# Values two steps behind their scores in the sliding attention, two taps a turn, sums of the last experts deferred, and three or four column tiles begun on half of the tokens

## The chip, the cores and the metric

The kernel runs on one core of a Trainium2 chip. Its engines are TensorE (PE in the profile, with PEld for its weight loads), VectorE (DVE), ScalarE (ACT), GpSimd (POOL) and SyncE (SP, which issues the DMAs). The metric is device time in microseconds of one execution of the whole program; the number to be compared is the median of the runs.

## The reference

Two transformer layers over 512 tokens of width 1024 run one after the other, all in float32. Cut to what the change touches:

```python
def first_block(x, ...):
    xn = rms_norm(h, g_mix); proj = xn @ w_in          # columns: conv 2*512, q 512, k 128, v 128, two gates of 1024
    conv_o = silu(layer_norm(depthwise_conv(a * sigmoid(gate), 31 taps))) @ w_conv_out
    attn_o = sliding_window_attention(q, k, v, sinks) @ w_attn_out   # 8 heads, 2 kv heads, window 128, blocks of 128
    h = h + (sigmoid(gate_conv) * conv_o + sigmoid(gate_attn) * attn_o) @ w_out
    h = h + hierarchical_moe(rms_norm(h, g_ffn), ...)  # 32 experts of 512, 2 per token
    return rms_norm(h, g_final)                        # and then the second layer:
def hybrid_layer(x, ...):
    h1 = rms_norm(x, mix_norm_gain); proj = h1 @ w_in_2              # gated delta rule and sparse attention
    ...
    x = x + merged @ w_out_2
    gate, up = split(rms_norm(x, ffn_norm_gain) @ w_gate_up_2)       # 2 x 2816 columns
    return x + (silu(gate) * up) @ w_down_2
```

In the sliding attention a block of 128 queries sees its own block of keys and the one before; scores get a bias by distance and a sink, then softmax, then the product with the values. In the experts' layer every token's output is the weighted sum of its two experts.

## The kernel before

The 512 tokens are four tiles of 128. A projection makes one column tile of 128 columns at a time for all 512 tokens: `mm3` (lines 327 to 329) writes every float32 product as three, high by high, high by low, low by high, over eight depth steps, 24 matmuls in all. A weight tile is therefore split ahead of use: ScalarE copies the high part (line 196), VectorE or GpSimd subtracts it from the raw weights (line 214). `plan` lists the column tiles in order; `fill_w` splits as many ahead as `look` says, and `next_w` takes one. Raw weights, splits, activations and experts' weights all live in a pool of 20 slots called `ck`; whoever asks for a slot waits until one is released, and DMAs on SP's queue wait in order. PSUM has eight banks, taken one at a time by `ps`. The program is written in one order; a planner with a cost model then orders each engine's instructions, except where `pe` or `keep_in_program_order` fix it or `issue_after` puts an instruction behind another on its engine.

Sliding attention (`swa`, lines 671 to 740): eight steps, one for each block of queries and half of the heads. `scores` does the products (line 692), bias (694), maximum (696), exponentials with sums (700) and scaling (706); `values` transposes the probabilities (717), copies them (719) and multiplies with the values (722). `values` of a step is issued after the scores of the next. `weave` (line 1368) calls the attention one turn at a time, and after every turn issues `pump` waiting convolution taps (line 572, VectorE, 31 per 128 channels) and one piece of `fill`, 12 matmuls of a projection tile. The fill's gates end in a tanh on ScalarE (line 664). After the attention come eight products with the attention's output weights (`branch`, line 621), each with four more taps if any wait, and then the convolution's norm, which needs the sum over all taps.

Experts (`moe`, lines 983 to 1018): 16 pairs of experts. For pair i the gate and up products run, then the down product of pair i-1 (`down`, which writes its output as high and low parts into the one tile `self.y`), and `combine` adds the output of pair i-2 to the tokens: for each of the four token tiles and two halves of the width two matmuls into a bank, and an addition into `h` on VectorE (line 1225). The weights stream in by DMA, 11 chunks of 1 MB ahead.

Start of the second layer (`block2`, lines 1278 to 1345): the sum of pair 15 runs tile by tile; after tiles 0 and 1 come squares (ScalarE, line 1287), the gain (line 1291), squares again, and `pair(0)`, which makes the product of two root-mean-square factors and multiplies (line 1307); the tiles are then transposed (`turn`, line 374). Tiles 2 and 3 follow; their gain runs on GpSimd. While `pair(1)` is made, `begin(2)` computes the first two column tiles for tokens 0 to 255 only, and `finish` does the other half after tiles 2 and 3 are turned.

Feed-forward start (`ffn_x`, `ffn_t`, `ffn_plan`, lines 1995 to 2032): the same pattern, one token tile at a time behind the output projection: norm (line 2007), turn, and before the last turn `begin(2)`. The raw weights of the first gate and up pair lie in `ck`, those of the later ones in a small pool `wf` of the last stage.

Of the kernel before, what the change touches and what calls it, by code (L numbers as in the profile page):

```python
# [8 lines left out]
F32R = mybir.dt.float32r  # L9
# [6 lines left out]
P = 128  # L16
# [136 lines left out]

AHEAD = 11


class Net:
# [336 lines left out]
    def phase_a(self):  # L494
# [120 lines left out]
        ath, atl = (self.ck([P, 4, 512], F32R) for _ in range(2))  # L615
        self.weave([self.swa(q, kv, ath, atl)], fill, pump=4)

# [53 lines left out]
    def swa(self, q, kv, ath, atl):  # L671
# [9 lines left out]
        def scores(qb, r2):  # L681
            nk = 128 if qb == 0 else 256
            k0 = max(qb - 1, 0) * P
            s = self.small([P, 4, 256], "sc", bufs=2)
            mx, nmx, sm, es = (self.small([P, 4], n) for n in ("mx", "nmx", "sm", "es"))
# [41 lines left out]

        steps = [(qb, r2) for qb in range(NT) for r2 in range(2)]
        prev = None
        for st in steps:  # L730
            s = scores(*st)
            yield
            if prev is not None:
                values(*prev)
                yield
            else:
                for _ in range(3):
                    yield
            prev = st + (s,)
        values(*prev)  # L740

# [241 lines left out]
    def moe(self):  # L983
# [5 lines left out]
        for i in range(16):  # L989
            q = quad[i // 2]  # L990
            back = self.combine(quad[i // 2 - 1], i % 2, ys.pop(i - 2)) if i > 1 else iter(())
            if i % 2 == 0:
# [18 lines left out]
            if i:  # L1011
                ys[i - 1] = self.down(i - 1, hT, quad[(i - 1) // 2])
        hT = self.turned(hms.pop(15))
        for _ in self.combine(quad[7], 0, ys.pop(14)):
            pass
        y = self.down(15, hT, quad[7])
        self.start_b()
        self.block2(quad.pop(7), y)

# [173 lines left out]

    def down(self, i, hT, q):

# [3 lines left out]
        for jj in range(2):  # L1199
# [7 lines left out]
            self.prefetch(self.used + AHEAD)  # L1207
        y = self.y
        for half in range(2):
# [3 lines left out]

    def combine(self, q, j, y, done=None):

        nc = self.nc
        mm = nc.tensor.matmul
        for t in range(NT):
            for half in range(2):
                fs = slice(half * 512, half * 512 + 512)  # L1220
                pc = self.ps()
                l = q["ohT"][:, j, t * P:(t + 1) * P]
                self.pe(mm, pc, l, y[:, 0, fs], start=True, stop=False)
                self.pe(mm, pc, l, y[:, 1, fs], start=False, stop=True)
                nc.vector.tensor_tensor(out=self.h[:, t, fs], in0=self.h[:, t, fs], in1=pc, op=ALU.add)  # L1225
                if half == 0:
                    yield
            if done:
                done(t)
            yield  # L1230
# [46 lines left out]

    def block2(self, q, y):

# [9 lines left out]
        def gained(t):  # L1289
            e = nc.gpsimd if t > 1 else nc.vector  # L1290
            e.tensor_tensor(out=self.h[:, t], in0=self.h[:, t], in1=self.rows[:, 0], op=ALU.mult)

        def pair(t2):

            s, v_, r_ = ss[t2], v[t2], r[t2]
            iv = self.small([P, 2], "iv")
            ts_(out=v_[:, 0], in0=s[:, 0], scalar1=1.0 / D, scalar2=EPS, op0=ALU.mult, op1=ALU.add)
            nc.vector.reciprocal(out=iv, in_=v_[:, 0])
            ts_(out=v_[:, 1], in0=s[:, 1], scalar1=1.0 / D, scalar2=None, op0=ALU.mult)
            nc.vector.tensor_tensor(out=v_[:, 1], in0=v_[:, 1], in1=iv, op=ALU.mult)  # L1300
            ts_(out=v_[:, 1], in0=v_[:, 1], scalar1=EPS, scalar2=None, op0=ALU.add)
            self.rsqrt(v_, r_)
            r12 = self.small([P, 2], "r12")
            nc.vector.tensor_tensor(out=r12, in0=r_[:, 0], in1=r_[:, 1], op=ALU.mult)
            for u in range(2):
                x, t = xs[t2][:, u], 2 * t2 + u
                last = nc.vector.scalar_tensor_tensor(out=x, in0=self.h[:, t], scalar=r12[:, u:u + 1], in1=self.rows[:, 1],
                                                      op0=ALU.mult, op1=ALU.mult)
            return self.root, last
# [3 lines left out]
        def done(t):  # L1313
            if t > 1:
                with self.tc.issue_after(first[0].ins):
                    squares(t, 0)
                gained(t)
                return
# [5 lines left out]

        for _ in self.combine(q, 1, y, done=done):
            pass
        self.fill_w()
        for t in (0, 1):
            last = self.turn(xs[0][:, t], t)
        with self.tc.issue_after(last[0].ins):  # L1330
            for t in (2, 3):
                squares(t, 1)
        with self.tc.issue_after(last[1].ins):
            pair(1)
        finish = self.begin(2)
        for t in (2, 3):
# [673 lines left out]
    def ffn_t(self, t):  # L2010
        if t == 1:
            self.look = 1
            self.fill_w()
            self.look = 0
        finish = self.begin(2) if t == NT - 1 else None
        self.turn(self.xs_of[t], t)
# [4 lines left out]
    def ffn_plan(self):  # L2021
# [3 lines left out]
        def wtile(f, a, box={}):  # L2025
            if a == 0:
                box["w"] = w = self.small([P, 2, KD, P], "wf") if f else self.ck([P, 2, KD, P])
                for b in range(2):
# [154 lines left out]
```

## Time and profile before

| what | value |
| --- | --- |
| median of 3 runs | 1784.6 us (1783.42 to 1784.62) |
| profiled execution, its own time | 1785.45 us |
| its span, first to last instruction | 1783.7 us |
| TensorE busy | 1716.4 us, 96% |
| VectorE, ScalarE, GpSimd busy | 827.6, 561.3, 332.4 us |
| mean granted TensorE clock | 0.985 of full speed |

The profile is of one execution. A row of idle time names the engine and line that released the waiting instruction. The granted clock is a share of 2.4 GHz; 0.50 is the lower level of 1.2 GHz, and a window with a value between the two holds both. Matmuls overlap at their ends, so the busy time of a stretch divided by its matmuls, and not the duration of one, is the pitch.

### The profile page before, as it was taken

Reading aid. Unit: us, or ns where it says so; the run is one execution under the profiler, and the core shown is the slowest. Engines: PE = TensorE matmul, PEld = TensorE weight load, DVE = VectorE, ACT = ScalarE, POOL = GpSimd, SP = SyncE. Lnnn points to the kernel's source line nnn. Section 1 sums busy time; section 2 is a strip of 40 time slices with the busy share of each in tenths; the row PEclk is TensorE's granted clock in tenths of the full one; section 3 lists DMA queues with packets and bytes.
Section 4 is the critical chain, followed back from the end, with each engine's and each line's share of the span. In section 5 each row is a group of like instructions: output and inputs, shape, how many; then the busy total and the mean of one; then the engine's idle time right before and its main releaser. Section 6 shows DMA issues by size and latency. Waiting matters only on the chain.

```text
span 1783.7 us, 21733 instructions
## 1 busy us (share of the span) xinstructions
PE 1716.4 (96%) x8672; PEld 1224.0 (69%) x8672; DVE 827.6 (46%) x1516; ACT 561.3 (31%) x1052; POOL 332.4 (19%) x208
## 2 busy tenths in 40 slices
PE   8998999999999999997999999899999899999998
PEld 6866888644444454434769988776578788888886
DVE  6996365723242333237576224556835422232222
ACT  4355254310101010104662234434523322332331
POOL 1000000000000000003327312321124133333450
PEclk9998999999999999998999999999999999999999
DMA  6221326599999999992311011210123233331431
GB/s 228 71 71 24 118 95 236 213 414 384 424 425 422 427 425 426 425 375 69 99 47 36 25 64 46 72 56 25 48 71 130 71 118 94 95 95 48 142 106 48
DMA packets 131594, 303.70 MB, mean 170 GB/s; under 512 B 5757, under 2 KB 90493, under 8 KB 106402
## 3 DMA queue, kind: packets, MB, share of 16 engines
q1 hardware_dynamic: 131490, 302.28, 45.1%
q8 instruction: 70, 1.15, 0.3%
q14 instruction: 34, 0.28, 0.0%
HBM read 300.16 MB, written 2.10 MB: 169 GB/s over the span
## 4 chain that ended last, share of the span: by engine, by line
PE 44%; DVE 5%; ACT 3%; issue 3%; POOL 1%; DVEq 0%; ACTq 0%; POOLq 0%
PE ps L327 8%; PE ps L328 8%; PE ps L329 8%; PE ps L2121 3%; PE ps L2120 3%; PE ps L2119 3%; PE ps L1607 1%; PE ps L1621 1%; PE ps L1156 1%; PE ps L1623 1%; PE ps L1926 1%; PE ps L1921 1%; PE ps L1903 1%; PE ps L1829 1%; DVE ck L1492 1%
## 5 line engine op out<-in xcount | busy, mean ns | idle before, releaser
L327 PE MATMUL ps<-ck,ck 128*128 128x512 f32 (+2 forms) x1112 | 438.0, 395 | 5.3 <-ACT ck L196 2.7
L328 PE MATMUL ps<-ck,ck 128*128 128x512 f32 (+2 forms) x1112 | 429.3, 387 | 1.1 <-DVE ck L336 1.1
L329 PE MATMUL ps<-ck,ck 128*128 128x512 f32 (+2 forms) x1112 | 427.4, 385 | 0.5 <-POOL ck L214 0.5
L327 PEld LDWEIGHTS ps<-ck,ck 128*128 128x128 f32 (+1 forms) x1112 | 210.2, 189 | 60.5 <-issue 10.2
L328 PEld LDWEIGHTS ps<-ck,ck 128*128 128x128 f32 (+1 forms) x1112 | 210.5, 189 | 48.3 <-issue 7.8
L329 PEld LDWEIGHTS ps<-ck,ck 128*128 128x128 f32 (+1 forms) x1112 | 210.4, 189 | 42.8 <-issue 1.5
L1156 PE MATMUL ps<-ck,ck 128*64 128x512 f32 x1024 | 226.3, 594 | 0.0
L214 POOL TENSOR_TENSOR ck<-ck,ck 128x512 fp32r<-128x512 f32 (+1 forms) x81 | 141.9, 1768 | 357.8 <-ACT ck L196 225.4
L1156 PEld LDWEIGHTS ps<-ck,ck 128*64 128x64 f32 x1024 | 72.0, 137 | 142.1 <-issue 135.8
L214 DVE TENSOR_TENSOR ck<-ck,ck 128x512 fp32r<-128x512 f32 (+1 forms) x109 | 110.8, 1036 | 91.1 <-PE ps L2120 44.2
L2119 PE MATMUL ps<-ck,ck 128*128 128x512 f32 x304 | 119.8, 395 | 0.0
L2121 PE MATMUL ps<-ck,ck 128*128 128x512 f32 x304 | 118.5, 390 | 0.0
L2120 PE MATMUL ps<-ck,ck 128*128 128x512 f32 x304 | 118.4, 390 | 0.0
L1156 PE MATMUL ps<-ck,hT 128*64 128x512 f32 x512 | 115.0, 602 | 2.0 <-PEq L1062 2.0
L1138 POOL TENSOR_TENSOR ohw<-oh,wt 128x512 f32<-128x512 f32 x16 | 16.5, 1050 | 470.2 <-issue 334.4
L214 POOL TENSOR_TENSOR ck<-wf,ck 128x1024 fp32r<-128x1024 f32 x28 | 77.3, 2791 | 143.4 <-ACT ck L196 143.4
L339 ACT ACTIVATE ck<-ps,ws 128x512 fp32r<-128x512 f32 x32 | 21.9, 687 | 253.9 <-PE ps L1156 253.9
L196 ACT ACTIVATE ck<-ck 128x1024 fp32r<-128x1024 f32 (+1 forms) x98 | 87.0, 911 | 13.7 <-PE ps L1921 4.2
L1156 PEld LDWEIGHTS ps<-ck,hT 128*64 128x64 f32 x512 | 36.4, 138 | 72.9 <-issue 63.0
L572 DVE SCALAR_TENSOR_TENSOR ck<-ck,wdw,ck 128x495 f32<-128x495 f32 (+23 forms) x120 | 83.8, 730 | 0.3
L1225 DVE TENSOR_TENSOR h<-h,ps 128x512 f32<-128x512 f32 x128 | 79.6, 678 | 6.9 <-PE ps L1156 6.9
L2051 DVE TENSOR_TENSOR sf<-ps,sf 128x512 f32<-128x512 f32 x22 | 15.2, 691 | 127.6 <-PE ps L329 127.6
(398 smaller groups left out, 2232.3 us busy)
## 6 DMA issues: line engine op xcount, KB each, us to landing
ck<-in_w_down SPq DMA_DIRECT2D x74, 1024.0 KB, 9.4
ck<-in_w_gate SPq DMA_DIRECT2D x64, 1024.0 KB, 11.2
ck<-in_w_up SPq DMA_DIRECT2D x64, 1024.0 KB, 9.3
ck<-in_w_in SPq DMA_DIRECT2D x34, 1024.0 KB, 5.1
wf<-in_w_gate_up SPq DMA_DIRECT2D x42, 512.0 KB, 4.8
ck<-in_w_out SPq DMA_DIRECT2D x8, 1024.0 KB, 4.9
h<-in_x SPq DMA_DIRECT2D x4, 512.0 KB, 6.5
ck<-in_w_in SPq DMA_DIRECT2D x4, 512.0 KB, 7.7
```

The source lines that it names most:

```text
L196: nc.scalar.activation(out=h, in_=src, func=AF.Copy)
L214: e.tensor_tensor(out=out, in0=src, in1=h.bitcast(F32), op=ALU.subtract)
L327: mm(ps, wh[:, k], xh[:, k, cols], start=k == 0, stop=False, skip_group_check=part)
L328: mm(ps, wh[:, k], xl[:, k, cols], start=False, stop=False, skip_group_check=part)
L329: mm(ps, wl[:, k], xh[:, k, cols], start=False, stop=k == K - 1, skip_group_check=part)
L339: nc.scalar.activation(out=h, in_=src, func=AF.Copy, scale=scale)
L572: nc.vector.scalar_tensor_tensor(out=y[:, c, o:], in0=v[:, c, :512 - o], scalar=wdw[:, c, 30 - o:31 - o], in1=y[:, c, o:], op0=ALU.mult, o ...
L1156: return self.tc.keep_in_program_order(f(*args, **kw))
L1225: nc.vector.tensor_tensor(out=self.h[:, t, fs], in0=self.h[:, t, fs], in1=pc, op=ALU.add)
L2119: mm(acc[t], ah[:, kk, ts], wh[:, k], start=kk == 0, stop=False)
L2120: mm(acc[t], ah[:, kk, ts], wl[:, k], start=False, stop=False)
L2121: mm(acc[t], al[:, kk, ts], wh[:, k], start=False, stop=kk == K - 1)
```

## The change

In the sliding attention the values of a step are issued two steps behind their scores, with a third buffer for scores, and two taps instead of four go out after every turn. In the experts' layer the outputs of pairs 13 and 15 get tiles of their own; the sums of pairs 13, 14 and 15 are made one by one only for token tiles 0 and 1, and for tiles 2 and 3 together at the end, six matmuls into a bank and one addition. In `block2` the gain of tiles 2 and 3 moves from GpSimd to VectorE, behind the turns of tiles 0 and 1, the factor of the two norms is computed as one root, and four column tiles instead of two are begun. At the feed-forward's start three are begun instead of two, with the second pair of raw weights loaded into `ck`.

```diff
-        self.weave([self.swa(q, kv, ath, atl)], fill, pump=4)
+        self.weave([self.swa(q, kv, ath, atl)], fill, pump=2)
...
-            s = self.small([P, 4, 256], "sc", bufs=2)
+            s = self.small([P, 4, 256], "sc", bufs=3)
...
-        steps = [(qb, r2) for qb in range(NT) for r2 in range(2)]
-        prev = None
-        for st in steps:
+        behind = deque()
+        for st in [(qb, r2) for qb in range(NT) for r2 in range(2)]:
             s = scores(*st)
             yield
-            if prev is not None:
-                values(*prev)
+            if len(behind) == 2:
+                values(*behind.popleft())
+            yield
+            if not any(st):
                 yield
-            else:
-                for _ in range(3):
-                    yield
-            prev = st + (s,)
-        values(*prev)
+                yield
+            behind.append(st + (s,))
+        values(*behind.popleft())
+        yield
+        values(*behind.popleft())
...
+LAST = (13, 14, 15)
...
-            back = self.combine(quad[i // 2 - 1], i % 2, ys.pop(i - 2)) if i > 1 else iter(())
+            back = self.combine(quad[i // 2 - 1], i % 2, ys[i - 2], range(2 if i - 2 in LAST else NT)) if i > 1 else iter(())
...
-                ys[i - 1] = self.down(i - 1, hT, quad[(i - 1) // 2])
+                ys[i - 1] = self.down(i - 1, hT, quad[(i - 1) // 2], self.ck([P, 2, D], F32R) if i - 1 == 13 else self.y)
         hT = self.turned(hms.pop(15))
-        for _ in self.combine(quad[7], 0, ys.pop(14)):
+        for _ in self.combine(quad[7], 0, ys[14], range(2)):
             pass
-        y = self.down(15, hT, quad[7])
+        ys[15] = self.down(15, hT, quad[7], self.ck([P, 2, D], F32R))
         self.start_b()
-        self.block2(quad.pop(7), y)
+        self.block2(quad, ys)
...
+    def combine_all(self, pairs, tiles, done=None):
...
-        for t in range(NT):
+        for t in tiles:
...
-                l = q["ohT"][:, j, t * P:(t + 1) * P]
-                self.pe(mm, pc, l, y[:, 0, fs], start=True, stop=False)
-                self.pe(mm, pc, l, y[:, 1, fs], start=False, stop=True)
+                for i, (l, y) in enumerate(pairs):
+                    for part in range(2):
+                        self.pe(mm, pc, l[:, t * P:(t + 1) * P], y[:, part, fs], start=i + part == 0, stop=part == 1 and i == len(pairs) - 1)
                 nc.vector.tensor_tensor(out=self.h[:, t, fs], in0=self.h[:, t, fs], in1=pc, op=ALU.add)
...
         def gained(t):
-            e = nc.gpsimd if t > 1 else nc.vector
-            e.tensor_tensor(out=self.h[:, t], in0=self.h[:, t], in1=self.rows[:, 0], op=ALU.mult)
+            nc.vector.tensor_tensor(out=self.h[:, t], in0=self.h[:, t], in1=self.rows[:, 0], op=ALU.mult)
...
-            iv = self.small([P, 2], "iv")
             ts_(out=v_[:, 0], in0=s[:, 0], scalar1=1.0 / D, scalar2=EPS, op0=ALU.mult, op1=ALU.add)
-            nc.vector.reciprocal(out=iv, in_=v_[:, 0])
-            ts_(out=v_[:, 1], in0=s[:, 1], scalar1=1.0 / D, scalar2=None, op0=ALU.mult)
-            nc.vector.tensor_tensor(out=v_[:, 1], in0=v_[:, 1], in1=iv, op=ALU.mult)
-            ts_(out=v_[:, 1], in0=v_[:, 1], scalar1=EPS, scalar2=None, op0=ALU.add)
+            ev = self.small([P, 2], "ev")
+            ts_(out=ev, in0=v_[:, 0], scalar1=EPS, scalar2=None, op0=ALU.mult)
+            nc.vector.scalar_tensor_tensor(out=v_[:, 1], in0=s[:, 1], scalar=1.0 / D, in1=ev, op0=ALU.mult, op1=ALU.add)
             self.rsqrt(v_, r_)
-            r12 = self.small([P, 2], "r12")
-            nc.vector.tensor_tensor(out=r12, in0=r_[:, 0], in1=r_[:, 1], op=ALU.mult)
+            r12 = r_[:, 1]
...
-        for _ in self.combine(q, 1, y, done=done):
+        for _ in self.combine(quad[7], 1, ys[15], range(2), done=done):
+            pass
+        for _ in self.combine_all([(quad[i // 2]["ohT"][:, i % 2], ys[i]) for i in LAST], range(2, NT), done=done):
             pass
         self.fill_w()
         for t in (0, 1):
             last = self.turn(xs[0][:, t], t)
+        with self.tc.issue_after(last[1].ins):
+            for t in (2, 3):
+                gained(t)
...
-        finish = self.begin(2)
+        finish = self.begin(4)
...
     def ffn_t(self, t):
         if t == 1:
-            self.look = 1
+            self.look = 2
             self.fill_w()
             self.look = 0
-        finish = self.begin(2) if t == NT - 1 else None
+        finish = self.begin(3) if t == NT - 1 else None
...
-                box["w"] = w = self.small([P, 2, KD, P], "wf") if f else self.ck([P, 2, KD, P])
+                box["w"] = w = self.small([P, 2, KD, P], "wf") if f > 1 else self.ck([P, 2, KD, P])
```

## Rows read from the trace of the kernel before

**Rows 1.** Part 1 of the page: busy time, share, instructions of each engine.

```profile
PE 1716.4 (96%) x8672; PEld 1224.0 (69%) x8672; DVE 827.6 (46%) x1516; ACT 561.3 (31%) x1052; POOL 332.4 (19%) x208
```

**Rows 2.** Waits of TensorE, whole span: total us, times, longest us.

```profile
PE ps L374 <- DVE ck L1307: 10.5, 2, 9.2
PE ps L717 <- ACT sc L706: 7.5, 3, 4.3
PE ps L327 <- ACT ck L196: 2.7, 2, 2.5
...
PE ps L722 <- ACT PT L719: 0.7, 1, 0.7
```

**Rows 3.** Windows: length; PE, PEld, DVE, ACT, POOL busy; clock; DMA share; GB/s.

```profile
89.20:133.80 44.60, 41.47 (x198) 28.61 (x197) 42.63 (x78) 22.70 (x63) 0.00 (x0) 1.00 0.25 71
...
136.00:139.00 3.00, 2.31 (x8) 0.84 (x7) 3.00 (x5) 2.44 (x5) 0.00 (x0) 0.50 0.03 5
139.00:143.50 4.50, 4.50 (x19) 2.42 (x18) 3.98 (x8) 3.19 (x12) 0.00 (x0) 0.50 0.00 0
...
163.20:166.50 3.30, 3.30 (x16) 2.33 (x16) 0.00 (x0) 2.17 (x5) 0.00 (x0) 0.69 1.06 248
...
178.40:223.00 44.60, 44.00 (x193) 35.75 (x191) 15.10 (x21) 11.87 (x19) 1.28 (x1) 1.00 0.36 118
```

**Rows 4.** Timeline, sliding attention: start, length, engine, line, count, [idle before <-releaser].

```profile
120.57 4.58 DVE L572 SCALAR_TENSOR_TENSOR ck<-ck,wdw,ck 128x508 f32<-128x508 f32 x7
...
131.54 0.60 ACT L664 ACTIVATE sg<-ps 128x512 f32<-128x512 f32 x1 [4.84 <-PE ps L329]
...
135.78 1.67 PE L717 MATMUL ps<-ident,sc 128*128 128x128 f32 x4 [4.28 <-ACT sc L706]
```

**Rows 5.** Timeline of TensorE, last experts' sums and the first turn.

```profile
779.11 2.12 PE L1156 MATMUL ps<-ck,ohT 128*128 128x512 f32 x8
...
814.17 4.17 PE L1156 MATMUL ps<-ck,ohT 128*128 128x512 f32 x15 [0.29 <-DVE ck L340]
827.54 1.97 PE L374 MATMUL ps<-ident,ck 128*128 128x128 f32 x8 [9.20 <-DVE ck L1307]
```

**Rows 6.** Timeline of VectorE, then of GpSimd, start of the second layer.

```profile
817.47 1.22 DVE L1291 TENSOR_TENSOR h<-h,ck 128x1024 f32<-128x1024 f32 x1
...
823.98 0.16 DVE L1304 TENSOR_TENSOR r<-b_r 128x2 f32<-128x2 f32 x1
824.17 6.60 DVE L1307 SCALAR_TENSOR_TENSOR ck<-h,r,ck 128x1024 f32<-128x1024 f32 x2
...
838.84 2.48 DVE L1307 SCALAR_TENSOR_TENSOR ck<-h,r,ck 128x1024 f32<-128x1024 f32 x2
...
824.05 5.64 POOL L1291 TENSOR_TENSOR h<-h,ck 128x1024 f32<-128x1024 f32 x2 [114.77 <-ACT ck L1287]
...
831.89 4.71 POOL L214 TENSOR_TENSOR ck<-ck,ck 128x1024 fp32r<-128x1024 f32 x2
```

**Rows 7.** Windows behind the first turn of the second layer.

```profile
827.50:833.00 5.50, 4.14 (x18) 3.44 (x18) 4.27 (x3) 1.62 (x4) 5.42 (x4) 0.50 0.00 0
833.00:837.00 4.00, 3.98 (x20) 3.10 (x20) 3.93 (x7) 2.62 (x6) 3.60 (x2) 0.52 0.00 0
```

**Rows 8.** The down weights' DMAs from 740 us on: issues, time to landing.

```profile
L794 SPq DMA_DIRECT2D ck<-in_w_down x10: 327/356/384, 742.2 to 775.8; - x10
...
DMA to landing us min/median/max: 10.0/16.5/19.5
```

**Rows 9.** Timeline of ScalarE and of TensorE, start of the feed-forward stage.

```profile
1424.55 5.78 ACT L196 ACTIVATE ck<-wf 128x1024 fp32r<-128x1024 f32 x6
...
1425.64 0.50 PE L327 MATMUL ps<-ck,ck 128*128 128x512 f32 x1 [2.46 <-ACT ck L196]
```

**Rows 10.** Window behind that wait.

```profile
1426.00:1431.00 5.00, 4.78 (x14) 3.51 (x13) 2.56 (x2) 4.33 (x5) 4.38 (x2) 0.66 0.09 26
```

More of the change, by code (lines that the diff above doesn't have):

```diff
@@ L1192, in turned, with down @@
         return hT
-    def down(self, i, hT, q):
+    def down(self, i, hT, q, y):
         nc = self.nc
@@ L1207, in down @@
             self.prefetch(self.used + AHEAD)
-        y = self.y
         for half in range(2):
@@ L1212, in down, with combine @@
         return y
-    def combine(self, q, j, y, done=None):
+    def combine(self, q, j, y, tiles, done=None):
+        return self.combine_all([(q["ohT"][:, j], y)], tiles, done)
+    def combine_all(self, pairs, tiles, done=None):
         nc = self.nc
         mm = nc.tensor.matmul
-        for t in range(NT):
+        for t in tiles:
             for half in range(2):
@@ L1276, in misc_w, with block2 @@
         return w[:, 0], w[:, 1]
-    def block2(self, q, y):
+    def block2(self, quad, ys):
         nc = self.nc
@@ L1316, in done @@
                     squares(t, 0)
-                gained(t)
                 return
```

## Prediction

> **What bounds the kernel now.** Part 1 of the page comes first: TensorE is busy 1716.4 of 1783.7 us [rows 1]. Every matrix product stays in the changed kernel, so at most the 67.3 us of idle time, and stretches at the lower clock, can go. The view of waits of TensorE says where that idle time lies [rows 2]: the transposes of line 374 wait 10.5 us in two waits for line 1307 (the start of the second layer), the transposes of line 717 wait 7.5 us in three waits for the scaled scores of line 706, and 0.7 us for line 719 (sliding attention), and line 327 waits 2.7 us for weights from line 196 (start of the feed-forward stage). These are the three places that the change edits. The windows then give the granted clock around each, since a wait is followed by matmuls at 1.2 instead of 2.4 GHz [rows 3, 7, 10], and the timelines say what the waiting instruction stood behind [rows 4 to 6, 9].
>
> **Sliding attention.** VectorE is busy 42.63 of 44.60 us there [rows 3], a good part of it with convolution taps of 4.58/7 = 0.65 us [rows 4]. The long wait is a queue: ScalarE sat 4.84 us until TensorE ended a piece, did its tanh (line 664), and only then the exponentials behind it; the transposes stood 4.28 us [rows 4]. Idle: 7.5 + 0.7 = 8.2 us. Clock: 2.31 us at 0.50 costs 1.2, 4.50 us at 0.50 costs 2.25, 3.30 us at 0.69 costs 1.0; together 4.4 [rows 3]. So 12.6 us can go.
> What the change gives: a piece of filling is 12 matmuls of 44.6/193 = 0.23 us, 2.8 us [rows 3]. Values now come five pieces after their scores instead of three, the last ones three instead of two: 5.6 us more time, 2.8 at the end, against waits of at most 4.3 us. And VectorE does four taps a step (a step is one scores and one values turn) instead of eight, 2.6 us less.
> What it moves: 31 taps wait when the attention starts and 32 operations join after eight pieces; 20 turns of two take 40, so 23 are left, 23 x 0.65 = 15.0 us. They go to the eight attention-output products behind it, where VectorE has 15.10 of 44.60 us to do [rows 3]: 30.1 fit. The weight subtractions there queue behind taps on VectorE, and TensorE needs them; I leave 1.6 us for that and for what stays of the waits. Were that cover gone, the 15.0 us would stand ahead of the convolution's norm. The third score buffer costs space alone. Bounds: +12.6 to 0 (the wait is the ScalarE queue's and stays), and below, as a rival. Taken: **11.0**, nearer the top because the added time exceeds the longest wait.
>
> **End of the experts and start of layer two.** Before, TensorE ends its last sum at 814.17 + 4.17 = 818.34 us and stands 9.20 until 827.54 [rows 5]; a second wait of 10.5 - 9.2 = 1.3 follows [rows 2]. Then it runs 4.14 us at 0.50 and 3.98 us at 0.52: 2.1 + 1.9 = 4.0 us lost [rows 7].
> The 9.2 us: the sums of token tiles 2 and 3 of experts' pairs 13 and 14 (8 matmuls each, 2.12 us [rows 5]) move behind those of tiles 0 and 1 of pair 15: 4.2 us of work goes into the hole and leaves the places where TensorE had no slack. The chain that ends the hole gets shorter: two multiplications of line 1307 took 6.60 us while GpSimd did line 1291 (two in 5.64), and 2.48 later without it [rows 6]. The first took half, 3.3, and becomes 1.24: 2.1 us less. After the last square one small VectorE operation stands where four stood (the eps terms, the product of roots), three at 0.19 us (the 0.16 operation at 823.98 to the next at 824.17) [rows 6]: 0.6. So 9.2 - 4.2 - 2.1 - 0.6 = 2.3 stay: gain 6.9. Of the 1.3, about 1.1 goes, as the second multiplication is as long as the eight transposes ahead of it. Of the 4.0 us of clock I leave 1.6, since an idle of about 2.4 us still lowered the clock elsewhere (4.78 us at 0.66 after the 2.46 [rows 9, 10]): gain 2.4. Sum **10.4**.
> The gain multiplications of tiles 2 and 3, now on VectorE, are 2 x 1.22 us [rows 6] in a new place: behind the turns, ahead of the second pair's root. From the end of the first pair of line 1307 (824.17 + 6.60) to the start of the second (838.84) was 8.1 us [rows 6]; with 2.4 more and 0.6 less 9.9, and 1.2 for the first product: 11.1. TensorE now has one turn (1.0) and four half-wide tiles, 4 x 24 x 0.115 = 11.0 us: 12.0 covers it, by 0.9. The two more begun tiles cost nothing in matmuls, they come out of the next stage. Their splits and one more weight load on SP's queue come earlier; the loads behind it on SP are for tiles needed 11 us later. The third column tile's split is the least covered, worth at most one 2.4 us GpSimd operation [rows 6].
> The two new sum tiles take ck slots. One is taken while weights stream, so the last loads are issued later by at most the 16 matmuls that free a pair, about 4 us. The last down weights were issued by 775.8 and landed within 19.5 us [rows 8]: 795.3, then 799. The last down product needs them 32 matmuls of 0.27 us before 814.17, less the 4.2 us moved: about 801. Nothing is lost, by 2 us. Combining six matmuls in one PSUM bank saves VectorE eight additions, off the path. Bounds of this part: 9.2 + 1.3 + 4.0 = 14.5, and -0.5 (the second rival).
>
> **Feed-forward start.** TensorE waited 2.46 us for the third half-tile's weights, which ScalarE split at 1424.55, behind the gate of the first [rows 9], 2.7 with a small one [rows 2]; then 4.78 us at 0.66 cost 1.6 [rows 10]. Sum 4.3. Now these weights are loaded into a ck slot and split during the output projection; the next ones are the fourth, asked for one tile later (5.5 us), with their raw data there already. That their split again stands behind the first gate's work on ScalarE can leave a short wait: I take **3.3**. Bounds 4.3 and -2.4 (one GpSimd subtraction late under a full ck pool).
>
> **Sum.** 11.0 + 10.4 + 3.3 = 24.7 us. The profiled execution took 1785.45 us (span 1783.7 and 1.75 around it), 0.85 over the median of 1784.6: 1785.45 - 24.7 = 1760.8, on the median's scale 1759.9. I say **1760**.
>
> **A rule that speaks against one edit.** Line 1307 and line 1291 held each other up [rows 6]: 6.60 us is the two multiplications' 2.48 and 4.1 of waiting. The Trainium skill, SBUF — State Buffer, section Who interferes with whom, says that a VectorE instruction with two SBUF inputs and a GpSimd instruction that reads SBUF exclude each other, whichever starts first holding the port to its end. By that rule, with which this trace agrees, moving the gain to VectorE does not take it out of the contest: the weight subtractions on GpSimd come forward into the freed time. By that rule alone the sum would be the second rival's 1771.
>
> **Rivals.**
> 1. Forecast, 0.60: 1760, its own range 1753 to 1767.
> 2. The port is fought over by others, 0.15. GpSimd's weight subtractions (4.71/2 = 2.36 us each [rows 6]) run where line 1291 ran. Line 1307 stays at 3.3, so the hole shrinks by 4.2 + 0.6 = 4.8 alone, the 1.3 stays and the clock's 4.0 with it; each gain multiplication waits 2.36, and 11.1 + 4.7 exceeds the cover of 12.0 by 3.8, with 1.5 of clock. 4.8 - 5.3 = -0.5 for the part, sum 13.8: 1771. For it: the 6.60. Against: GpSimd had only 4.71 us of them, and they wait for ScalarE.
> 3. The attention does not gain, 0.13: its waits are ScalarE's order, which the planner writes anew, not the lag. Sum 13.7: 1771. For it: the 4.84 us behind line 664. Against: the lag gives more than the wait.
> 4. Slower, 0.07: the same place, made worse. With three score buffers the planner lets tanh or PT copies, which wait for TensorE, stand ahead of exponentials in more steps. Each such wait costs 4.3 and 3.4 of clock, 7.7 us [rows 3, 4]. Four of them, 30.8, are 18.2 more than today's 12.6, less 13.7 from the other parts: 4.5 slower, 1789; six of them 1804. It decides from four on. For it: one such wait stands in the trace. Against: VectorE, which makes the scores late, gets less to do.
> 5. No change, 0.05: rivals 2 and 3 together, 0 - 0.5 + 3.3 = 2.8 us: 1782.
>
> A measurement of this kernel tells about 0.2%, 3.6 us, from no change. Faster: 0.60 + 0.15 + 0.13 = 0.88; same 0.05; slower 0.07. The range goes up to cover the rivals at 1771 with room, and down to a little past where all of 12.6 + 14.5 + 4.3 = 31.4 us is won (1753): 1752 to 1775.
>
> **What would show it.** Right: no wait of line 717 for line 706 over 1 us and a clock near 1.00 from 131 to 169 us; taps among the attention-output products; TensorE's hole before the first turn of layer two at about 2 us, line 1307's first pair near 2.5 us; no wait for line 196 at the feed-forward start. Wrong: line 1307 again above 3 us each beside line 214 on GpSimd; a wait of line 374 after the four begun tiles; a new wait of TensorE for line 214 in the products behind the attention; the hole kept at over 4 us; down products waiting for their weights.

## The result, and the profile after

The changed kernel takes 1769.42 us (median of 4 runs, 1767.53 to 1770.74) against 1784.24 us of the kernel before on the same chip (4 runs, 1783.42 to 1784.62): ratio 0.9915, 95% interval 0.9900 to 0.9929. That is 14.8 us, inside the predicted range of 1752 to 1775 us, but 60% of the 24.7 us that were forecast. Run again later beside the kernel before (experiment 12), it gained 12.5 us. The profiled execution spans 1768.5 us, 15.2 less than the one before. Part 1 of the page, TensorE's row, answers to [rows 1]:

```profile
PE 1709.0 (97%) x8744; PEld 1226.0 (69%) x8744; DVE 826.6 (47%) x1504; ACT 560.9 (32%) x1052; POOL 326.7 (18%) x206
```

The waits of TensorE over the whole span (total, times, longest) answer to [rows 2]; `mm3` is now lines 328 to 330, `turn` line 375, the products of the two norms line 1311:

```profile
PE ps L375 <- DVE ck L2015: 4.2, 3, 2.8
...
PE ps L375 <- DVE ck L1311: 3.2, 2, 3.0
...
PE ps L723 <- ACT PT L720: 1.0, 2, 0.7
```

The 10.5 us for the second layer's start have become 3.2, the 7.5 us for the scaled scores are gone, and the 2.7 us for line 196 as well. But a wait of the feed-forward start for line 2015, its norm, is new at 2.8 us.

To see where the time went, the span is cut at the same matmuls in both kernels. This table is the ledger that some expectations below speak of. First the windows of the kernel before, then those of the changed one (start and end, length, busy PE, PEld, DVE, ACT, POOL, clock, DMA share, GB/s): the program's start, the sliding attention with the products behind it, the last pair of experts, the start of layer two, the last turn of the delta rule's scan, the feed-forward start.

```profile
0.00:58.70 58.70, 50.73 (x252) 41.46 (x253) 43.23 (x79) 24.36 (x38) 7.77 (x16) 1.00 0.58 191
58.70:210.50 151.80, 143.60 (x662) 106.39 (x661) 114.79 (x201) 67.82 (x164) 0.00 (x0) 0.96 0.24 73
771.70:813.40 41.70, 39.10 (x171) 16.24 (x167) 14.34 (x23) 4.00 (x7) 0.00 (x0) 0.96 0.79 312
813.40:881.60 68.20, 56.01 (x281) 43.32 (x279) 49.69 (x82) 38.06 (x60) 30.88 (x22) 0.90 0.22 69
1074.30:1145.50 71.20, 66.30 (x351) 55.19 (x350) 32.71 (x62) 31.92 (x69) 23.64 (x14) 0.98 0.20 60
1392.60:1651.20 258.60, 253.59 (x1167) 210.56 (x1167) 80.17 (x86) 77.12 (x104) 82.07 (x30) 0.99 0.30 90
```

```profile
0.00:60.50 60.50, 50.64 (x252) 41.70 (x253) 43.13 (x79) 24.36 (x38) 7.76 (x16) 0.97 0.56 185
60.50:197.70 137.20, 136.07 (x661) 103.17 (x660) 116.13 (x201) 67.62 (x164) 0.00 (x0) 1.00 0.28 80
757.50:797.90 40.40, 35.71 (x154) 13.28 (x150) 9.63 (x14) 4.37 (x7) 1.23 (x2) 0.96 0.79 312
797.90:863.70 65.80, 59.75 (x344) 49.10 (x342) 46.30 (x78) 38.31 (x60) 23.67 (x18) 0.95 0.26 79
1055.00:1128.20 73.20, 67.22 (x350) 55.85 (x349) 33.77 (x62) 31.91 (x69) 23.60 (x14) 0.95 0.18 58
1375.30:1636.00 260.70, 254.98 (x1190) 213.30 (x1190) 85.53 (x86) 76.99 (x104) 82.45 (x30) 0.99 0.29 85
```

Attention: 14.6 us less (11.0 forecast). Last experts and start of layer two: 1.3 + 2.4 = 3.7 less (10.4 forecast). Feed-forward start: 2.1 *more* (3.3 less forecast). Program's start and last scan turn, which nothing edits: 1.8 and 2.0 more. The stretches not shown give 2.8 back with 0.4 us less idle time, so nearly all of it is TensorE's busy time for the same matmuls: 15.2 in all.

**Last experts.** Timeline of the changed kernel, ScalarE and then TensorE (start, length, engine, line, operation, [idle before <-releaser]):

```profile
764.64 0.60 ACT L1184 ACTIVATE sil<-ps 128x512 f32<-128x512 f32 x1 [25.66 <-PE ps L1160]
765.19 0.60 ACT L347 ACTIVATE hT<-ps 128x512 f32<-128x512 f32 x1
765.69 1.26 ACT L340 ACTIVATE ck<-ps,ws 128x512 fp32r<-128x512 f32 x2
```

```profile
757.53 7.04 PE L1160 MATMUL ps<-ck,ck 128*64 128x512 f32 x32
...
766.42 0.49 PE L1160 MATMUL ps<-ck,ohT 128*128 128x512 f32 x1 [1.26 <-ACT ck L340]
767.21 2.86 PE L1160 MATMUL ps<-ck,ohT 128*128 128x512 f32 x7 [0.29 <-DVE ck L341]
```

Pair 13's down product is done when pair 15's gate product begins, at 757.53. ScalarE is idle then, yet copies that output (line 340) only at 765.69, behind the silu of pair 15. TensorE waits for it, and runs at a mean clock of 0.89 from 762 to 777 us. The 16 matmuls that left this stretch (4.2 us) so shorten it by 1.3. In the kernel before, where the output went into the shared tile, the first of the two copies ran at 771.09, ahead of the silu, as soon as TensorE let it:

```profile
771.09 0.69 ACT L339 ACTIVATE ck<-ps,ws 128x512 fp32r<-128x512 f32 x1 [17.91 <-PE ps L1156]
```

**Start of layer two.** TensorE's first turn, then VectorE's first pair of products:

```profile
809.63 2.61 PE L375 MATMUL ps<-ident,ck 128*128 128x128 f32 x11 [2.98 <-DVE ck L1311]
```

```profile
808.29 2.48 DVE L1311 SCALAR_TENSOR_TENSOR ck<-h,b_r,ck 128x1024 f32<-128x1024 f32 x2
```

The hole (TensorE's wait ahead of this turn) is 2.98 us where 9.20 stood [rows 5], and the two products take 2.48 where they took 6.60 [rows 6].

**Feed-forward start.** ScalarE, VectorE, GpSimd and TensorE of the changed kernel:

```profile
1386.03 2.01 ACT L197 ACTIVATE ck<-ck 128x1024 fp32r<-128x1024 f32 x2
1387.93 1.06 ACT L353 ACTIVATE ck<-h 128x1024 f32<-128x1024 f32 x1
```

```profile
1388.07 2.59 DVE L215 TENSOR_TENSOR ck<-ck,ck 128x1024 fp32r<-128x1024 f32 x1 [1.10 <-ACT ck L197]
1390.59 0.14 DVE L359 TENSOR_SCALAR v<-ss 128x1 f32<-128x1 f32 x1
...
1392.40 1.28 DVE L2015 SCALAR_TENSOR_TENSOR ck<-h,r,ck 128x1024 f32<-128x1024 f32 x1
```

```profile
1387.17 2.41 POOL L215 TENSOR_TENSOR ck<-ck,ck 128x1024 fp32r<-128x1024 f32 x1 [4.19 <-ACT ck L197]
```

```profile
1393.74 1.97 PE L375 MATMUL ps<-ident,ck 128*128 128x128 f32 x8 [2.81 <-DVE ck L2015]
```

The third column tile's split (the second of the two at line 197, and line 215) stands ahead of token tile 2's square (353) and norm (359) on both engines, so tile 2 is turned late: the wait has changed its place, from 2.46 us for weights [rows 9] to 2.81 us for the norm. Part of the lateness is a meeting of two splits: VectorE's subtraction took 2.59 us while GpSimd did that of the second tile (1387.17 to 1389.58), and 1.22 in experiment 5, where it ran alone.

### The profile page after: what moved, and what is told of

Its sections match the earlier page's. It is cut to its first block, busy times and chain, and to the rows that moved or that the text cites. A ratio compares the mean times of both kernels' runs of the same rounds, so it can differ in the third digit from the quotient of the medians.

```text
span 1768.5 us, 21848 instructions
## 1 busy us (share of the span) xinstructions
PE 1709.0 (97%) x8744; PEld 1226.0 (69%) x8744; DVE 826.6 (47%) x1504; ACT 560.9 (32%) x1052; POOL 326.7 (18%) x206
## 4 chain that ended last, share of the span: by engine, by line
PE 41%; issue 6%; DVE 5%; ACT 3%; POOL 1%; DMA 1%; POOLq 0%; ACTq 0%; DVEq 0%
PE ps L328 8%; PE ps L329 8%; PE ps L330 8%; PE ps L2127 2%; PE ps L2129 2%; PE ps L2128 2%; PE ps L1615 1%; PE ps L1160 1%; PE ps L1629 1%; POOL ck L215 1%; PE ps L1631 1%; PE ps L1934 1%; PE ps L1929 1%; PE ps L1911 1%; DVE ck L1500 1%
## 5 line engine op out<-in xcount | busy, mean ns | idle before, releaser
L328 PEld LDWEIGHTS ps<-ck,ck 128*128 128x128 f32 (+1 forms) x1136 | 215.1, 190 | 57.9 <-issue 10.4
L329 PEld LDWEIGHTS ps<-ck,ck 128*128 128x128 f32 (+1 forms) x1136 | 215.9, 190 | 47.0 <-issue 8.2
L330 PEld LDWEIGHTS ps<-ck,ck 128*128 128x128 f32 (+1 forms) x1136 | 215.4, 190 | 42.6 <-POOL ck L215 2.3
L1232 DVE TENSOR_TENSOR h<-h,ps 128x512 f32<-128x512 f32 x120 | 74.8, 678 | 0.6 <-PE ps L1160 0.6
L2059 DVE TENSOR_TENSOR sf<-ps,sf 128x512 f32<-128x512 f32 x22 | 15.2, 690 | 124.6 <-PE ps L330 123.0
```

The costliest lines, as they stand in the source:

```text
L328: mm(ps, wh[:, k], xh[:, k, cols], start=k == 0, stop=False, skip_group_check=part)
L329: mm(ps, wh[:, k], xl[:, k, cols], start=False, stop=False, skip_group_check=part)
L330: mm(ps, wl[:, k], xh[:, k, cols], start=False, stop=k == K - 1, skip_group_check=part)
```

## The experiments

Unless it is said otherwise, each starts from the changed kernel. Times are medians; each comes with its ratio to the kernel before, run on the same chip, and the 95% interval. Stretches are cut at the same matmuls as above, and each is read from one profile. Cut lines of an edit are marked by three dots.

**1. Attention alone**, on the kernel before: the lag (the rewritten loop of steps), the third buffer, two taps.

```diff
-            s = self.small([P, 4, 256], "sc", bufs=2)
+            s = self.small([P, 4, 256], "sc", bufs=3)
...
-        self.weave([self.swa(q, kv, ath, atl)], fill, pump=4)
+        self.weave([self.swa(q, kv, ath, atl)], fill, pump=2)
```

> The kernel before with the edits of the sliding attention alone (values two steps behind, a third buffer of scores, two taps a turn). Theory, by the ledger of the two traces: the stretch from the attention's start to the end of the products behind it gives back its whole 8.2 us of idle time and the lower clock, 14.6 us, and 1.8 us at the start of the program (a wait for the first split weights, 2.64 in place of 1.06 us) belong to these edits too or do not: 1784.2 - 14.6 = 1769.6, with the 1.8 us 1771.4. Rival, the prediction's own 11.0 us with a remainder of waits for the scaled scores or the weight subtractions: 1773. Rival, the attention gains only with the other parts: above 1776.

Measured: 1771.35 us, 0.9927 (0.9913 to 0.9940). The attention stretch takes 137.16 us, as in the changed kernel; the last experts and the start of layer two take what they took before, to 0.1 us. The 14.6 us belong to this part alone (the medians differ by 14.8), and it makes nearly all of the result. The start takes 60.4 us.

**2 and 3. Which of the two attention edits?** On the kernel before: experiment 2 has the loop and the buffer, with four taps a turn; experiment 3 has the last line of that diff alone.

> The kernel before with the lag alone: values two steps behind and a third buffer of scores, but four taps a turn as before. Theory (the lag removes the waits, the taps only help): the stretch from the attention to the end of the products behind it, 151.73 us before and 137.16 us with both edits, comes to 137 to 140 us; 1771 to 1774 in all. Rival (VectorE's taps made the scaled scores late): it keeps most of its waits, over 146 us, 1780 or more.

> The kernel before with two taps a turn instead of four, and the values one step behind as before. Theory (the lag is needed, because ScalarE's order stands between the maximum and the scaled scores): about half of the waits stay, 144 to 148 us for the stretch of 151.73, 1777 to 1781 in all. Rival (taps alone): 137 to 139 us for the stretch, 1772.

Measured: lag 1779.53 us, 0.9967 (0.9956 to 0.9978), stretch 143.99; taps 1773.62, 0.9932 (0.9917 to 0.9948), stretch 138.14. The theory fell: in the stretch the taps alone bring 13.6 of the 14.6 us, the lag alone 7.7; in the medians 10.7 and 4.8 of 14.8. TensorE's idle time in the stretch, 8.2 us before, is 1.3 with the taps, 4.6 with the lag and 1.1 in the changed kernel. The view of one line shows why: the scaling of the scores, first and last start, in the kernel before, with the lag, with the taps, and in the changed kernel (there line 707):

```profile
L706 ACT ACTIVATE sc<-sc,sm x32: 384/494/510, 88.0 to 163.8; 128x256 f32<-128x256 f32 x24, 128x128 f32<-128x128 f32 x8
```

```profile
L706 ACT ACTIVATE sc<-sc,sm x32: 384/495/511, 89.1 to 157.8; 128x256 f32<-128x256 f32 x24, 128x128 f32<-128x128 f32 x8
```

```profile
L706 ACT ACTIVATE sc<-sc,sm x32: 387/494/510, 89.0 to 152.8; 128x256 f32<-128x256 f32 x24, 128x128 f32<-128x128 f32 x8
```

```profile
L707 ACT ACTIVATE sc<-sc,sm x32: 384/496/511, 89.8 to 151.0; 128x256 f32<-128x256 f32 x24, 128x128 f32<-128x128 f32 x8
```

The eight steps' scaled scores take 75.8 us before, 68.7 with the lag, 63.8 with the taps, 61.2 with both. VectorE, 42.63 of 44.60 us busy [rows 3], paces the softmax, and each tap between maximum and sums makes every later step later. It is the place of the taps that counts, not their number: in all as many run, and in the changed kernel VectorE is as busy, 31.23 of 32.00 us, where TensorE hardly waits:

```profile
128.00:160.00 32.00, 31.16 (x165) 21.86 (x166) 31.23 (x56) 20.78 (x57) 0.00 (x0) 1.00 0.16 34
```

I read the 4.84 us that ScalarE stood behind a tanh as how one late step looked, not as the limit. That is argued: with fewer taps the planner also wrote ScalarE's order anew (in experiment 3 the tanh at 131.31 us stands behind a step's exponentials, in the kernel before the one at 131.54 ahead of them), and no run holds that order fixed.

**4. Feed-forward start undone:**

```diff
-            self.look = 2
+            self.look = 1
...
-        finish = self.begin(3) if t == NT - 1 else None
+        finish = self.begin(2) if t == NT - 1 else None
...
-                box["w"] = w = self.small([P, 2, KD, P], "wf") if f > 1 else self.ck([P, 2, KD, P])
+                box["w"] = w = self.small([P, 2, KD, P], "wf") if f else self.ck([P, 2, KD, P])
```

> The changed kernel with the feed-forward start as it was (two column tiles begun, one split ahead, the raw weights of the second pair in the small pool). Theory: this part of the change costs, because the third tile's split stands ahead of the norm of token tile 2 on ScalarE and VectorE; the stretch falls back by 2.1 us: 1769.4 - 2.1 = 1767.3, with the wait of 2.46 us for line 197 back. Rival, the prediction's step: the change gains 3.3 us there and the 2.1 us in the ledger come from elsewhere: 1772.7.

Measured: 1768.35 us, 0.9903 (0.9888 to 0.9918): no difference from the changed kernel that can be told. From the last output products to the next stage it takes 264.24 us, as before (264.20; this cut ends some 5 us later than the window above, which had 258.60); the changed kernel 266.34 in its first profile. That figure was at the dear end: six further profiles with the new start unmended have 263.6 to 265.2, all with 5.7 to 5.8 us idle, where the old start has 5.0 (5.3 in experiment 3), so the part as built is worth between +0.6 and -2.1 us, and -0.6 in the mean of the seven; by the idle time it loses some 0.7.

**5. The third split later**, its raw weights still loaded at token tile 1:

```diff
-        if t == 1:
-            self.look = 2
+        if t in (1, 2):
+            self.look = t
             self.fill_w()
             self.look = 0
+        if t == 1:
+            self.ffn_load(1)
...
```

`ffn_load` is the loading of a pair's raw weights, taken out of the function that splits them.

> The changed kernel with the third column tile's raw weights still loaded early, but its split asked for one token tile later, so that it stands behind the norm of token tile 2. Theory: the 2.81 us wait of the transposes falls to some 0.5 us, and the lower clock behind it (0.50 over 4.3 us, 2.1 us) goes: 2.3 + 2.1 = 4.4, 1765.0; the fourth tile's 1.2 us of waits stay. Rival: the split is then late for the third begun tile itself, which waits 2 to 3 us for line 197 or 215: 1769, no gain.

Measured: 1766.10 us, 0.9886 (0.9871 to 0.9901); the stretch 261.21, 5.1 less than in the first profile and 3.0 less than before. VectorE has the norm's product (2015) ahead of the subtraction (215), and the turn hardly waits:

```profile
1393.41 1.29 DVE L2015 SCALAR_TENSOR_TENSOR ck<-h,r,ck 128x1024 f32<-128x1024 f32 x1
1394.61 1.22 DVE L215 TENSOR_TENSOR ck<-ck,ck 128x1024 fp32r<-128x1024 f32 x1
```

```profile
1394.75 1.09 PE L375 MATMUL ps<-ident,ck 128*128 128x128 f32 x8 [0.42 <-DVE ck L2015]
```

The harm lay in the place of the split, ahead of the norm and beside GpSimd's, and not in loading its weights early.

**6. Pair 13's copies first:**

```diff
-            nc.scalar.activation(out=h, in_=src, func=AF.Copy, scale=scale)
+            self.high = nc.scalar.activation(out=h, in_=src, func=AF.Copy, scale=scale)
...
+            with self.tc.issue_after(self.high.ins) if i == 15 else nullcontext():
...
```

The block holds pair 14's transposes, pair 13's sums and pair 15's silu.

> The changed kernel with ScalarE's silu of pair 15 and the copy of pair 14's transposed activations put behind the two copies of pair 13's output. Its tile stays where it is asked for. Theory: only the planner's order holds these copies back (ScalarE stands idle for 25.66 us ahead of that silu), so they run at about 758 instead of 765.69 us; TensorE's waits of 1.26 and 0.29 us go, and the clock of 0.89 over 15 us behind them, 1.6: 3.1 us, 1766.3. Rival: the tile's slot is not free before pair 15's gate weights are read, at 764.5 us; then the copies come no earlier, silu and copy queue behind them, and the time is 1769.4 to 1771.

Measured: 1766.74 us, 0.9900 (0.9885 to 0.9915). ScalarE's copies are line 341 here, the silu line 1186:

```profile
756.41 0.69 ACT L341 ACTIVATE ck<-ps,ws 128x512 fp32r<-128x512 f32 x1 [17.91 <-PE ps L1162]
757.29 0.69 ACT L341 ACTIVATE ck<-ps,ws 128x512 fp32r<-128x512 f32 x1 [0.20 <-PE ps L1162]
764.76 0.60 ACT L348 ACTIVATE hT<-ps 128x512 f32<-128x512 f32 x1 [6.78 <-PE ps L1162]
765.25 0.59 ACT L1186 ACTIVATE sil<-ps 128x512 f32<-128x512 f32 x1
```

```profile
756.90:793.20 36.30, 33.33 (x154) 12.78 (x150) 9.56 (x14) 3.85 (x7) 1.22 (x2) 1.00 0.88 346
```

They wait for TensorE's product alone and start some 9 us sooner, so the slot was free; only the order held them. The stretch falls from 40.4 to 36.4 us (1.7 of it idle, the rest clock, now 1.00). Together with the start of layer two it falls from 106.2 (106.1 in experiment 12) to 100.6 us, so the late copies cost 5.6 us in all.

**7 and 8. Sums in place:** only pair 15's sums of tiles 2 and 3 remain at the end.

```diff
-LAST = (13, 14, 15)
+LAST = (15,)
-                ys[i - 1] = self.down(..., self.ck([P, 2, D], F32R) if i - 1 == 13 else self.y)
+                ys[i - 1] = self.down(..., self.y)
```

> The changed kernel with the sums of pairs 13 and 14 made for all four token tiles where they were, so that only pair 15's remain at the end and pair 13 writes into the shared tile as before. Theory: the deferral's 4.2 us of matmuls in the hole are paid back by the late copies of pair 13's output (4.0 us in the experiment that put them first), so the undoing is worth nothing: TensorE's wait at line 375 grows from 2.98 to 7.2 us, the waits of 1.26 and 0.29 us go; 1769 to 1771. Rival, the prediction's step (the deferral gains its 4.2 us whole and pair 13's tile costs nothing): 1773.6 or more, with some clock 1775.

Experiment 7 leaves out pair 14's sums for token tiles 2 and 3, 8 matmuls, so its time is not that of the whole work; experiment 8 has them (`range(NT)` for pair 14).

> As the earlier experiment with the sums in place, now with pair 14's sums for all four token tiles. Theory: the 8 matmuls that were left out there add 2.1 us ahead of the last down product, 1765.9 + 2.1 = 1768.0: the deferral as it stands gains nothing. Rival, the prediction's step (its 4.2 us whole): 1773.6.

Measured: 1765.88 us, 0.9890 (0.9875 to 0.9905), and whole 1769.02, 0.9910 (0.9894 to 0.9925). The first turn's wait in the whole one:

```profile
PE ps L375 <- DVE ck L1311: 6.4, 1, 6.4
```

So the deferral does take 3.4 us out of the hole (6.4 to 2.98). But as it stands it gains nothing: the two stretches are 105.5 us together without it and 106.2 with it. With the copies first they are 100.6 (experiments 6 and 11): then it is worth 5.0. The medians agree, but less sharply: experiment 6 is 19.45 us below the kernel before beside it, experiment 8 15.45, with intervals that overlap.

**9. The gain of tiles 2 and 3 back on GpSimd**, issued behind the first squares as before:

```diff
-            nc.vector.tensor_tensor(out=self.h[:, t], ...)
+            e = nc.gpsimd if t > 1 else nc.vector
+            e.tensor_tensor(out=self.h[:, t], ...)
...
```

> The changed kernel with the gain of token tiles 2 and 3 back on GpSimd and issued where it was. Theory, the prediction's step: line 1311's first pair goes from 2.48 to about 6.6 us, the second half of it off the path, and the wait ahead of the first turn from 2.98 to about 5.1 us, with up to 1 us of clock: 1771.5 to 1772.5. Rival (the port was not what held it, or GpSimd's weight subtractions had already taken its place): 1769.4, no difference.

Measured: 1775.62 us, 0.9941 (0.9928 to 0.9955), 3.7 to 6.2 slower than the changed kernel's two medians. GpSimd, VectorE and TensorE (line 1312 here):

```profile
810.33 4.65 POOL L1298 TENSOR_TENSOR h<-h,ck 128x1024 f32<-128x1024 f32 x2 [114.32 <-ACT ck L1294]
```

```profile
810.48 2.23 DVE L396 TENSOR_SCALAR nt<-nt 128x4 f32<-128x4 f32 x1
812.74 2.26 DVE L397 TENSOR_TENSOR b_r<-b_r,nt 128x4 f32<-128x4 f32 x1
```

```profile
816.48 2.85 PE L375 MATMUL ps<-ident,ck 128*128 128x128 f32 x12 [7.25 <-DVE ck L1312]
```

GpSimd's two multiplications now meet the root's two small operations, 128x4, which take 2.23 and 2.26 us instead of 0.17 and 0.16. All of it stands on the path (7.25 against 2.98), where the prediction gave this edit 2.1, half of the pair at line 1307. One of the two has a single SBUF tensor as input; the Trainium skill, SBUF — State Buffer, section Who interferes with whom, lists `tensor_scalar` among the operations that can enter a two-port mode, which takes the port pair that VectorE shares with GpSimd, and with that the trace agrees.

**10. Two column tiles begun instead of four**, on experiment 6:

```diff
-        finish = self.begin(4)
+        finish = self.begin(2)
```

> The changed kernel with the copies of pair 13's output first and only two column tiles begun at the start of layer two, as before. Theory (the prediction's cover: two tiles less are 48 x 0.115 = 5.5 us less work ahead of the second turn): the turn of tiles 2 and 3 waits 4 to 5 us for line 1311, and the clock behind it costs 1 to 2: 6 us over the experiment that has the copies first, 1772 to 1773. Rival (the splits of the two extra tiles on VectorE and GpSimd are what makes the second pair late, so it comes earlier without them): 2 us or less, 1768.

Measured: 1765.55 us, 0.9893 (0.9877 to 0.9909), not to be told from experiment 6. TensorE waits 6.8 us in two waits for the norm's products instead of 3.5, but the 1.4 us that it waits for GpSimd's squares (line 1505) with four begun tiles are gone; the stretch is 2.5 us longer. The theory of 6 us fell. The rival holds in its mechanism: from the end of the first pair of products (line 1313) to the start of the second it takes 11.2 us, and 13.2 in experiment 6, where one of the root's small operations takes 2.17 us beside GpSimd's split of a begun tile, and 0.16 here. Its price of 2 us is near the 2.5 of the stretch; the medians show no loss.

```profile
PE ps L376 <- DVE ck L1313: 6.8, 2, 3.8
```

**11. Orders mended together**: experiments 5 and 6, and the fourth tile's split asked for earlier:

```diff
         self.turn(self.xs_of[t], t)
         if finish:
+            self.fill_w()
             finish()
```

> The changed kernel with three orders mended: the copies of pair 13's output first, the third column tile's split of the feed-forward start behind the norm of token tile 2, and the fourth tile's split asked for before the second half of the three begun tiles. Theory: the gains of the two earlier experiments add up, 4.0 us at the experts' end and 5.1 us at the feed-forward start in the ledger, and the fourth tile's waits of 0.18 and 1.00 us go: 10.3 us, 1769.4 - 10.3 = 1759. Rival: the clock takes back what the waits give (its level after a wait differs from run to run by up to 1.6 us a stretch), or the fourth split delays the third's: 1762 to 1765.

Measured: 1760.78 us (4 runs, 1759.09 to 1761.64), 0.9863 (0.9848 to 0.9878), the fastest of all, and 8.6 to 11.2 under the changed kernel's two medians (10.3 expected). The forecast's 24.7 us are 23.7 here, against the kernel before beside it. Its windows for last experts, start of layer two and feed-forward start (the first two begin and end some 0.6 us ahead of those matmuls; the third is the longer cut of experiment 4, 264.20 before):

```profile
757.90:794.20 36.30, 33.32 (x154) 12.94 (x152) 9.56 (x14) 3.85 (x7) 1.22 (x2) 1.00 0.87 345
794.20:858.40 64.20, 58.19 (x342) 47.39 (x339) 46.25 (x78) 38.67 (x60) 23.68 (x18) 0.97 0.26 81
1372.10:1631.40 259.30, 257.23 (x1216) 215.24 (x1215) 85.17 (x90) 79.77 (x109) 87.12 (x32) 1.00 0.30 89
```

**12. The changed kernel once more.**

> The changed kernel as it is, once more, beside the others on the same chip. Theory: the program's start (60.55 us to the first transposes of the attention, 58.75 before) and the last turn of the delta rule's scan (73.24 us, 71.21 before) differ between executions of one program, by a weight transfer's landing and the clock: the one falls to 59 to 60.7, the other to between 71.2 and 72.8, with a total of 1767 to 1771. Rival (the change moved them): both come again within 0.3 us.

Measured: 1771.95 us (5 runs, 1767.10 to 1772.92), 0.9925 (0.9911 to 0.9939). The start takes 60.2 us. In the thirteen profiles with any of the changes it lies between 59.1 and 60.7 us, and the instructions of TensorE, VectorE, ScalarE and GpSimd stand in the same order there as before; the 58.75 us of the kernel before are one profile. I count its 1.8 us as no effect of the change, though one profile is thin evidence. The last scan turn comes again at 73.2 us, against the theory; others of these kernels have 71.2. Some 1.1 us of the 2.0 are one wait of TensorE for VectorE's line 1712, 4.7 us here and 3.6 in the kernel before; why it is longer stays open.

## Why the prediction was right or wrong

**The number.** That it falls in the range is in part luck. 1769.4 us lies outside the forecast's own 1753 to 1767, and the second median, 1771.95, lies next to the 1771 of rivals 2 and 3, for which the range was drawn wide. Yet neither of them came true: the attention gained more than forecast, and line 1311's pair met nobody. One part's surplus of 3.6 us stood against two that fell short.

**Sliding attention: 11.0 forecast, 14.6 measured.** The waits went, as said. The reason was half wrong: the lag was to give the time, the halved taps to help, and it is the other way round. The clock's term was too small: TensorE's busy time fell by 7.5 us with the same matmuls, where 4.4 was counted. And that 23 taps go to the products did not come true in time: the planner ran all but one of them before VectorE took up the first of the eight products (162.54 us), so the cover that was weighed there was hardly needed. Rivals 3 and 4, which put the wait down to ScalarE's order, did not come true in their times. That the lag is not what counts was right in rival 3; whether ScalarE's order had a part is not shown, since experiment 3 changes it along with the taps.

**End of the experts and layer two: 10.4 forecast, 3.7 measured.** The hole is 2.98 us for 2.3, the second wait is nearly gone, the pair at line 1311 is free of the contest, the last down weights came in time. The step that failed is "Nothing is lost, by 2 us" on the new tile: it asked only whether the weights come later. Nobody asked where ScalarE's copies into that tile would stand. In the shared tile they stand right behind the product; a tile of its own let the planner put them behind pair 15's silu. That alone is 5.6 us over the two stretches; with it mended the part gives 9.3. "The two more begun tiles cost nothing" missed the 1.4 us for GpSimd's squares, which come with four begun tiles and not with two (experiment 10); why is not shown. The second rival had the right resource: GpSimd's subtractions do meet VectorE in the new place (line 394 takes 2.17 us), but under the begun tiles, which leave a second wait of 0.2 us.

**Feed-forward start: 3.3 less forecast; measured 2.1 more in the first profile, 0.6 more in the mean of seven.** The step that failed is that the third split, "loaded into a ck slot and split during the output projection", was entered at nothing, with no name for the work that would hide it. ScalarE and VectorE were in the norm of token tile 2 just then. Its lower bound, a subtraction late by 2.4 us, had the size right but the wrong victim. Behind the norm it gives 3.0 us, with the fourth split 4.9.

So 1760 was within reach of these edits, and experiment 11 gets there, with one order mended that the forecast did not have and with an attention that gives more than its share. The changed kernel stopped at 1769 for two orders that the forecast did not follow: ScalarE's copies at the end of the experts, and a split on ScalarE and VectorE at the feed-forward start.

## What to carry to other kernels

When a buffer is split off to relax a dependence, ask what else the old dependence did: it may have been what kept a copy early. When work is moved "ahead, under cover", write down on each engine the instruction it now stands in front of, and who waits for that. And where an engine is over 95% busy in a stage, look first at which of its work stands ahead of what others wait for: side work can move behind it without getting less.

## What the runs showed of the hardware

The same wait of 2.81 us ahead of the same turn was followed by half the clock in one execution of the changed kernel and by the full one in the other; the windows right behind it, first profile and experiment 12:

```profile
1393.70:1398.00 4.30, 4.26 (x20) 4.26 (x21) 3.24 (x8) 1.40 (x3) 0.00 (x0) 0.50 0.07 19
```

```profile
1393.20:1397.50 4.30, 4.23 (x36) 4.23 (x37) 3.27 (x9) 1.29 (x3) 0.00 (x0) 1.00 0.08 17
```

The stretch differs by 2.7 us for it (266.3 and 263.6) with equal idle time. A part worth 2 us can't be judged by one profile's clock; idle time can: with the start as built it repeats to 0.1 us in seven profiles, with the old one to 0.3 in five.
